# Products on 64 rows take turns between the two row halves of TensorE: attention scores by pairs of groups, selection scores, mixer scores

## The chip, the cores and the metric

One core of a Trainium2 chip runs the whole program in one launch. The time is the device time of one execution in microseconds (us), the median over runs. The engines have instruction streams of their own and run them in order: TensorE (PE, with a queue of weight loads beside its products), VectorE (DVE), ScalarE (ACT), GpSimd (POOL) and SyncE (SP). They meet at semaphores. Products are accumulated in PSUM, eight banks of 512 f32 columns by 128 partitions, and DVE or ACT carries them from there into SBUF.

## The reference, cut to what matters

The reference is a model of two blocks at 256 positions of width 1024. The first block has two layers: a mixer (a recurrence, attention with six heads and a position bias, and a state space part), then a layer that selects experts. The second has a recurrent mixer, an MLP, a sparse attention (NSA) with 16 heads in four groups, an MLP and a norm. Three kinds of product in it have 64 as the contracted dimension:

```python
# mixer attention: 6 heads of 64
s = jnp.einsum('bghnid,bghnjd->bghnij', qb, kw) + bias
# selection: 8 heads, each query in two halves of 64, each half against 128 sub-keys
q = (xt @ w_query).reshape(T, H, 2, PEER_HALF)
s = jnp.einsum('thcd,cnd->thcn', q, sub_keys)
sv, si = lax.top_k(s, K)
# NSA: 4 groups of 4 heads of 64; s_s (selected blocks) and s_w (window) for the same query
s_c = jnp.einsum('qghd,ngd->ghqn', qf, kc) - slopes * d_c      # 15 compressed keys
p_c = _masked_softmax(s_c, d_c >= 0)
s_s = jnp.einsum('qghd,gqkd->ghqk', qf, k_sel) - slopes * d_s
p_s = _masked_softmax(s_s, m_s)
s_w = jnp.einsum('qghd,kgd->ghqk', qf, kw) - slopes * d_w
p_w = _masked_softmax(s_w, m_w)
o = g[..., 0:1] * o_c + g[..., 1:2] * o_s + g[..., 2:3] * o_w
```

With 256 positions all four blocks of 64 are selected and the window holds everything, so that s_s and s_w are causal scores against two sets of keys.

## The kernel before, in words

Weights come as f32 from HBM, 512 KB at a time. ACT casts such a chunk to a high part (`hi`, L271), DVE subtracts it for the low part (`lo`, L273), and PE makes three products of each (`feat_mm`, L289, for results with features on partitions; `tok_mm`, L303, L305, L307, for results with tokens on partitions). This fills most of PE's time.

The program is written in an order of calls, and a list scheduler puts the instructions of each engine into the order in which they run. That order is fixed when the kernel is built. PSUM banks come from three pools: tag `a` (two banks), `acc` (four) and `g` (two). A tile of a pool gets its buffer when an earlier one is released.

Queries and keys lie with their features on partitions. Two heads (or two groups, or two halves of a query) share the 128 partitions: one on rows 0 to 63, the other on 64 to 127. A product on one half uses 64 rows of PE's array.

- **Mixer** (L671): for each token tile t of 128, the three even heads' scores into banks of `acc`, then the three odd heads'. DVE adds the bias (L673).
- **Selection** (`scores(t)`, L1046): for four heads at a time the first halves of their queries into one bank, then the second halves into the next. DVE then finds the 16 largest (L909 to L913).
- **NSA** (`attend(g, t)`, L1427): for a group g and a token tile t four heads' scores against two sets of keys, 256 columns a product for t=0 and 512 for t=1. They go into banks of tag `a`: two products a bank for t=0, one for t=1. DVE adds the position term (L1429) into the tile `ns` (three buffers), takes the maximum over keys (L1431), ACT takes eight exponentials (L1434), DVE multiplies by gate over sum (L1435 to L1439), PE transposes the result into banks of tag `g` (L1445), and ACT copies them to `pT` (L1447). `outputs(g)` multiplies them by the values (L1462, L1463), together with the compressed part (L1466).

Around it stand the calls of `nsa`: `query(i)` (24 products L289 with one weight chunk and a copy to `nq` on ACT, L1295) and `key`, `compressed(pr)` (scores against 15 compressed keys for eight heads: products L1384, softmax in the tile `sc`, weights `pc`, four transposes L1406, copy to `pcT` L1407), and `out(k)` (a weight chunk of the output, 12 products of `tok_mm`). A list `done` has the last exponential of each softmax; the high cast of a chunk of `query`, `key` and `out` is issued behind an entry of it:

```python
def project(i, tag=("a",)):
    if done: self.behind = done[-2:][:1]
    wh, wl = self.chunk(a["nsa_w_f"][i])
```

Of the kernel before, what the change touches and what calls it, by code (L numbers as in the profile page):

```python
# [16 lines left out]
OP = mybir.AluOpType  # L17
# [4 lines left out]
P = 128  # L22
# [159 lines left out]
class K:  # L182
# [446 lines left out]
    def attention(self, l, pool, u):  # L629
# [26 lines left out]
        for t in range(NT):  # L656
# [7 lines left out]
            for odd in range(2):  # L664
                rr = slice(odd * 64, odd * 64 + 64)
                for g0 in range(0, 3, per):
                    ng = min(per, 3 - g0)
                    b = self.bank("acc", 4)
                    for i in range(ng):
                        g = g0 + i  # L670
                        nc.tensor.matmul(b[:, i * w:(i + 1) * w], qkT[rr, g, t * P:(t + 1) * P], qkT[rr, 3 + g, :w],  # L671
                                         start=True, stop=True)
                    nc.vector.tensor_tensor(pv[:, g0:g0 + ng, odd], b[:, :ng * w].rearrange("p (h s) -> p h s", h=ng),  # L673
                                            rv[:, g0:g0 + ng, odd, S - w:], op=OP.add)
# [360 lines left out]
    def select(self, sp, qT, keys, sel, gates):  # L1035
# [4 lines left out]
        def scores(t):  # L1040
            banks = []
            for h4 in range(2):
                for c in range(2):
                    b = self.bank("acc", 4)
                    for j in range(4):
                        nc.tensor.matmul(b[:, j * P:(j + 1) * P], qT[c * 64:c * 64 + 64, 4 * h4 + j, t * P:(t + 1) * P],  # L1046
                                         keys[c * 64:c * 64 + 64, :], start=True, stop=True)
                    banks.append(b)
            return banks
# [215 lines left out]
    def nsa(self):  # L1265
# [3 lines left out]
        with tc.tile_pool(name="nsa", bufs=1) as pool:  # L1269
# [143 lines left out]
            def attend(g, t):  # L1413
                r = slice((g % 2) * 64, (g % 2) * 64 + 64)
                c0 = 4 * (g // 2)
                w = P * (t + 1)
                per = 512 // (2 * w)
                if t == 0:
                    for sb in range(2):
                        pT[g, sb] = T(f"pT{sb}", [P, 2, 4, S if sb == 0 else P], bufs=2)  # L1420
                s = T("ns", [P, 4, 2, S], bufs=3).rearrange("p h b s -> p (h b s)")[:, :8 * w].rearrange("p (h b s) -> p h b s", h=4, b=2)
                mx, sm = T("nmx", [P, 4, 2], bufs=3), T("nsm", [P, 4, 2], bufs=3)
                for h0 in range(0, 4, per):
                    b = self.bank("a")
                    bv = b.rearrange("p (h b s) -> p h b s", h=per, b=2)
                    for hh in range(h0, h0 + per):
                        nc.tensor.matmul(bv[:, hh - h0], qT[r, c0 + hh, t * P:(t + 1) * P], kT[r, g // 2, :, :w], start=True, stop=True)  # L1427
                    for hh in range(h0, h0 + per):
                        nc.vector.scalar_tensor_tensor(s[:, hh], alibi[:, None, S - w:].to_broadcast([P, 2, w]), slopes[4 * g + hh],  # L1429
                                                       bv[:, hh - h0], op0=OP.mult, op1=OP.add)  # L1430
# [6 lines left out]
                for hh in range(4):  # L1437
                    for br in range(2):
                        dv = nc.vector.tensor_scalar(s[:, hh, br], s[:, hh, br], sm[:, hh, br:br + 1], None, op0=OP.mult)  # L1439
                done.append((ex, dv if 0 else None))  # L1440
# [44 lines left out]
            compressed(0)  # L1485
            attend(0, 1)
            query(5)
            attend(1, 0)
            query(6)
            attend(1, 1)  # L1490
            outputs(0, ("acc", 4))
# [3 lines left out]
            attend(2, 0)  # L1495
# [3 lines left out]
            attend(2, 1)  # L1499
            out(1)  # L1500
            attend(3, 0)
            out(2)
            outputs(2, ("g",))
            attend(3, 1)
            out(3)
# [56 lines left out]
```

## Time and profile before

| | us |
|---|---|
| median of 3 runs | 2577.31 (2576.77 to 2577.53) |
| profiled execution | 2573.22 |
| its span, first to last instruction | 2571.4 |
| PE busy in it | 2493.8 (97%) |
| DVE busy | 1810.5 (70%) |
| ACT busy | 1202.0 (47%) |
| score products L1427 (NSA), L1046 (selection), L671 (mixer) | 64, 128 and 48 records |
| NSA, from the first L1427 to the L336 that close it | 104.83 |

A product of f32 tiles shows as two records of MATMUL in the trace. Busy time counts overlapping records once. A row of the timeline puts equal records one after another together: its start, the time until the last of them ends, their count, and in brackets how long the engine had been idle before the first of them and who ended that.

### The profile page before, as it was taken

The numbers are of one execution on the slowest core, as the hardware profiler recorded it, in microseconds if no ns is written. First come the engines' busy times: TensorE is split into PE (matmuls) and PEld (weight loads), VectorE is DVE, ScalarE is ACT, GpSimd is POOL, SyncE is SP. The second block draws the span as 40 slices with busy tenths as digits, with TensorE's granted clock in tenths as the row PEclk, the third lists the DMA queues.
The fourth block names the chain that finished last, engine by engine and source line by source line (L and its number), as shares of the span: only waits on it lengthen the run. The fifth ranks groups of instructions, "written<-read, shape, count | busy, mean of one in ns | idle before, by whom it ended". The sixth has DMA issues, their size and how long they took to land.

```text
span 2571.4 us, 44923 instructions
## 1 busy us (share of the span) xinstructions
PE 2493.8 (97%) x18200; PEld 2227.4 (87%) x18200; DVE 1810.5 (70%) x3138; ACT 1202.0 (47%) x1761; POOL 72.3 (3%) x79
## 2 busy tenths in 40 slices
PE   6999999999999998999999999999999999999998
PEld 5779999989978886889999989978879799886997
DVE  6768969964596557859968954696568655656655
ACT  5544443344434445544443444434447444455444
POOL 4000000000000003000000000000000000000000
PEclk9999999999999998999999999999999999999999
DMA  7235555465545664344554465545555555621564
GB/s 232 83 117 166 171 189 165 149 196 188 174 156 185 193 195 163 99 133 155 180 189 157 157 196 188 165 164 189 191 179 172 172 187 187 188 77 61 189 188 148
DMA packets 122072, 426.30 MB, mean 166 GB/s; under 512 B 14748, under 2 KB 18696, under 8 KB 121736
## 3 DMA queue, kind: packets, MB, share of 16 engines
q1 hardware_dynamic: 120448, 421.64, 51.3%
q8 instruction: 142, 2.33, 0.4%
q10 hardware_dynamic: 1416, 1.79, 0.2%
q14 instruction: 66, 0.54, 0.1%
HBM read 421.83 MB, written 2.24 MB: 165 GB/s over the span
## 4 chain that ended last, share of the span: by engine, by line
PE 48%; DVE 7%; ACT 1%; issue 1%; POOL 0%; DMA 0%; POOLq 0%; DVEq 0%; ACTq 0%
PE psa L289 19%; PE psacc L303 7%; PE psacc L307 7%; PE psacc L305 7%; DVE lo L273 2%; PE psacc L289 2%; PE psg L1004 1%; PE psa L1427 1%; PE psacc L300 1%; DVE tk L911 0%; PE psg L1445 0%; PE psacc L404 0%; DVE si L913 0%; ACT hi L271 0%; DVE x_sb L339 0%
## 5 line engine op out<-in xcount | busy, mean ns | idle before, releaser
L273 DVE TENSOR_TENSOR lo<-raw,hi 128x1024 fp32r<-128x1024 f32 (+1 forms) x778 | 942.7, 1219 | 494.1 <-ACT hi L271 493.6
L271 ACT CAST hi<-raw 128x1024 fp32r<-128x1024 f32 (+1 forms) x778 | 810.7, 1044 | 949.2 <-PE psa L289 512.0
L289 PE MATMUL psa<-xh,hi 128*128 128x256 f32 x2960 | 839.3, 288 | 2.4 <-DVE rst L241 1.7
L289 PE MATMUL psa<-xh,lo 128*128 128x256 f32 x2960 | 833.3, 285 | 2.4 <-DVE lo L273 2.3
L289 PE MATMUL psa<-xl,hi 128*128 128x256 f32 x2960 | 828.3, 283 | 0.0
L289 PEld LDWEIGHTS psa<-xh,hi 128*128 128x128 f32 x2960 | 569.4, 195 | 8.1 <-ACT xy L710 2.1
L289 PEld LDWEIGHTS psa<-xh,lo 128*128 128x128 f32 x2960 | 567.1, 193 | 6.1 <-DVE lo L273 5.6
L289 PEld LDWEIGHTS psa<-xl,hi 128*128 128x128 f32 x2960 | 563.8, 192 | 2.5
L303 PE MATMUL psacc<-hi,ch 128*128 128x512 f32 x984 | 305.6, 392 | 0.1
L305 PE MATMUL psacc<-lo,ch 128*128 128x512 f32 x984 | 303.6, 390 | 0.0
L307 PE MATMUL psacc<-hi,cl 128*128 128x512 f32 x984 | 302.8, 389 | 0.4 <-DVE cl L975 0.4
L307 PEld LDWEIGHTS psacc<-hi,cl 128*128 128x128 f32 x984 | 184.6, 188 | 40.1 <-DVE cl L975 1.2
L305 PEld LDWEIGHTS psacc<-lo,ch 128*128 128x128 f32 x984 | 184.7, 188 | 38.8
L303 PEld LDWEIGHTS psacc<-hi,ch 128*128 128x128 f32 x984 | 182.5, 188 | 36.3
L974 ACT CAST ch<-ca 128x512 fp32r<-128x512 f32 x124 | 77.0, 623 | 140.4 <-PE psacc L305 138.1
L975 DVE TENSOR_TENSOR cl<-ca,ch 128x512 fp32r<-128x512 f32 x124 | 85.7, 693 | 59.4 <-ACT ch L974 59.1
L1008 DVE TENSOR_TENSOR ca<-psg,ca 128x512 f32<-128x512 f32 x128 | 82.5, 688 | 15.2 <-PE psg L1004 15.2
L994 DVE TENSOR_TENSOR pg<-o,selg 128x1024 f16<-128x1024 f16 x128 | 82.8, 690 | 0.0
L376 POOL TENSOR_TENSOR ns<-ns,mhalf 128x1 f32<-128x1 f32 x18 | 15.9, 881 | 2231.4 <-DVE ns L375 2229.1
L989 DVE TENSOR_TENSOR o<-iota,sel 128x2048 f16<-128x2048 f16 x64 | 78.0, 1219 | 0.0
L303 PE MATMUL psacc<-hi,muh 128*128 128x512 f32 x248 | 77.3, 393 | 0.0
L305 PE MATMUL psacc<-lo,muh 128*128 128x512 f32 x248 | 76.8, 390 | 0.0
(411 smaller groups left out, 2663.9 us busy)
## 6 DMA issues: line engine op xcount, KB each, us to landing
raw<-in_down SPq DMA_DIRECT2D x256, 512.0 KB, 3.5
raw<-in_up SPq DMA_DIRECT2D x256, 512.0 KB, 3.5
raw<-in_mlp_up SPq DMA_DIRECT2D x64, 512.0 KB, 3.5
raw<-in_mlp_down SPq DMA_DIRECT2D x64, 512.0 KB, 3.5
raw<-in_w_in_t SPq DMA_DIRECT2D x32, 512.0 KB, 4.4
raw<-in_w_in_f SPq DMA_DIRECT2D x22, 512.0 KB, 4.3
raw<-in_w_out SPq DMA_DIRECT2D x16, 512.0 KB, 3.8
raw<-in_w_query SPq DMA_DIRECT2D x16, 512.0 KB, 3.5
```

Of the source, the lines that this page charges most:

```text
L271: nc.scalar.copy(hi, src)
L273: nc.vector.tensor_sub(lo, src, hi)
L289: nc.tensor.matmul(ps, w[:, k], x[:, k], start=i == 0, stop=i == len(seq) - 1)
L300: nc.tensor.matmul(acc[t][n][:, :w], xh[:, xs], wh[:, off[n]:off[n] + w], start=first, stop=last)
L303: nc.tensor.matmul(acc[t][n][:, :w], xh[:, xs], wh[:, off[n]:off[n] + w], start=first, stop=False)
L305: nc.tensor.matmul(acc[t][n][:, :w], xh[:, xs], wl[:, off[n]:off[n] + w], start=False, stop=False)
L307: nc.tensor.matmul(acc[t][n][:, :w], xl[:, xs], wh[:, off[n]:off[n] + w], start=False, stop=last)
L974: nc.scalar.copy(ch.rearrange("p b t -> p (b t)"), src)
L975: nc.vector.tensor_sub(cl.rearrange("p b t -> p (b t)"), src, ch.rearrange("p b t -> p (b t)"))
L989: nc.vector.tensor_tensor(pairs(o2), pairs(of(0, 64)), twice(si[:, 1], 64), op=OP.is_equal)
L994: nc.vector.tensor_tensor(pairs(pg[:, i]), pairs(o1), twice(sg[:, i], 32), op=OP.mult)
L1008: nc.vector.tensor_tensor(v, bk.rearrange("p (t i) -> p i t", t=8), v, op=OP.mult)
```

## The change

Mixer: one loop over the column groups, in which even and odd heads' products take turns, each half in a bank of its own. Selection: the same for the two halves of the queries. NSA: `attend(c, t)` now takes a pair of groups, 2c on rows 0 to 63 and 2c+1 on rows 64 to 127. Their products take turns into two banks of tag `a`; the additions on DVE follow, and then the two softmaxes, one after the other, in a function of their own. There are four calls of `attend` in place of eight, and the calls around it have another order. The amount of work is the same.

```diff
--- before.py
+++ after.py
@@ -661,16 +661,18 @@
             sm = pool.tile([P, 6], F32, tag="asm", name=self.nm("asm"), bufs=2)
             pv = p.rearrange("p (g two) s -> p g two s", two=2)
             rv = self.relb.rearrange("p (g two) s -> p g two s", two=2)
-            for odd in range(2):
-                rr = slice(odd * 64, odd * 64 + 64)
-                for g0 in range(0, 3, per):
-                    ng = min(per, 3 - g0)
-                    b = self.bank("acc", 4)
-                    for i in range(ng):
-                        g = g0 + i
-                        nc.tensor.matmul(b[:, i * w:(i + 1) * w], qkT[rr, g, t * P:(t + 1) * P], qkT[rr, 3 + g, :w],
+            for g0 in range(0, 3, per):
+                ng = min(per, 3 - g0)
+                bs = [self.bank("acc", 4) for _ in range(2)]
+                for i in range(ng):
+                    g = g0 + i
+
+                    for odd in range(2):
+                        rr = slice(odd * 64, odd * 64 + 64)
+                        nc.tensor.matmul(bs[odd][:, i * w:(i + 1) * w], qkT[rr, g, t * P:(t + 1) * P], qkT[rr, 3 + g, :w],
                                          start=True, stop=True)
-                    nc.vector.tensor_tensor(pv[:, g0:g0 + ng, odd], b[:, :ng * w].rearrange("p (h s) -> p h s", h=ng),
+                for odd in range(2):
+                    nc.vector.tensor_tensor(pv[:, g0:g0 + ng, odd], bs[odd][:, :ng * w].rearrange("p (h s) -> p h s", h=ng),
                                             rv[:, g0:g0 + ng, odd, S - w:], op=OP.add)
             nc.vector.tensor_reduce(mx, p, axis=AX.X, op=OP.max, negate=True)
             for h in range(6):
@@ -1040,12 +1042,13 @@
         def scores(t):
             banks = []
             for h4 in range(2):
-                for c in range(2):
-                    b = self.bank("acc", 4)
-                    for j in range(4):
-                        nc.tensor.matmul(b[:, j * P:(j + 1) * P], qT[c * 64:c * 64 + 64, 4 * h4 + j, t * P:(t + 1) * P],
+                bs = [self.bank("acc", 4) for _ in range(2)]
+                for j in range(4):
+
+                    for c in range(2):
+                        nc.tensor.matmul(bs[c][:, j * P:(j + 1) * P], qT[c * 64:c * 64 + 64, 4 * h4 + j, t * P:(t + 1) * P],
                                          keys[c * 64:c * 64 + 64, :], start=True, stop=True)
-                    banks.append(b)
+                banks += bs
             return banks
 
         ix = sp.tile([P, 2, NT, 8, 16], F32, tag="ix", name=self.nm("ix"))
@@ -1410,24 +1413,31 @@
             slopes = [2.0 ** (-8.0 * (h + 1) / 16) for h in range(16)]
             pT = {}
 
-            def attend(g, t):
-                r = slice((g % 2) * 64, (g % 2) * 64 + 64)
-                c0 = 4 * (g // 2)
+            def attend(c, t):
+
                 w = P * (t + 1)
                 per = 512 // (2 * w)
-                if t == 0:
-                    for sb in range(2):
-                        pT[g, sb] = T(f"pT{sb}", [P, 2, 4, S if sb == 0 else P], bufs=2)
-                s = T("ns", [P, 4, 2, S], bufs=3).rearrange("p h b s -> p (h b s)")[:, :8 * w].rearrange("p (h b s) -> p h b s", h=4, b=2)
+                ss = []
+                for g in (2 * c, 2 * c + 1):
+                    if t == 0:
+                        for sb in range(2):
+                            pT[g, sb] = T(f"pT{sb}", [P, 2, 4, S if sb == 0 else P], bufs=2)
+                    ss.append(T("ns", [P, 4, 2, S], bufs=3).rearrange("p h b s -> p (h b s)")[:, :8 * w].rearrange("p (h b s) -> p h b s", h=4, b=2))
+                for h0 in range(0, 4, per):
+                    bvs = [self.bank("a").rearrange("p (h b s) -> p h b s", h=per, b=2) for _ in range(2)]
+                    for hh in range(h0, h0 + per):
+                        for i in range(2):
+                            r = slice(i * 64, i * 64 + 64)
+                            nc.tensor.matmul(bvs[i][:, hh - h0], qT[r, 4 * c + hh, t * P:(t + 1) * P], kT[r, c, :, :w], start=True, stop=True)
+                    for i in range(2):
+                        for hh in range(h0, h0 + per):
+                            nc.vector.scalar_tensor_tensor(ss[i][:, hh], alibi[:, None, S - w:].to_broadcast([P, 2, w]),
+                                                           slopes[4 * (2 * c + i) + hh], bvs[i][:, hh - h0], op0=OP.mult, op1=OP.add)
+                for i in range(2):
+                    softmax(2 * c + i, t, ss[i])
+
+            def softmax(g, t, s):
                 mx, sm = T("nmx", [P, 4, 2], bufs=3), T("nsm", [P, 4, 2], bufs=3)
-                for h0 in range(0, 4, per):
-                    b = self.bank("a")
-                    bv = b.rearrange("p (h b s) -> p h b s", h=per, b=2)
-                    for hh in range(h0, h0 + per):
-                        nc.tensor.matmul(bv[:, hh - h0], qT[r, c0 + hh, t * P:(t + 1) * P], kT[r, g // 2, :, :w], start=True, stop=True)
-                    for hh in range(h0, h0 + per):
-                        nc.vector.scalar_tensor_tensor(s[:, hh], alibi[:, None, S - w:].to_broadcast([P, 2, w]), slopes[4 * g + hh],
-                                                       bv[:, hh - h0], op0=OP.mult, op1=OP.add)
                 nc.vector.tensor_reduce(mx, s, axis=AX.X, op=OP.max, negate=True)
                 for hh in range(4):
                     for br in range(2):
@@ -1436,8 +1446,8 @@
                 nc.vector.tensor_tensor(sm, sm, gv[:, t, 4 * g:4 * g + 4, 1:3], op=OP.mult)
                 for hh in range(4):
                     for br in range(2):
-                        dv = nc.vector.tensor_scalar(s[:, hh, br], s[:, hh, br], sm[:, hh, br:br + 1], None, op0=OP.mult)
-                done.append((ex, dv if 0 else None))
+                        nc.vector.tensor_scalar(s[:, hh, br], s[:, hh, br], sm[:, hh, br:br + 1], None, op0=OP.mult)
+                done.append((ex, None))
                 for br in range(2):
                     for sb in range(t + 1):
                         b = self.bank("g")
@@ -1483,26 +1493,22 @@
             attend(0, 0)
             query(4)
             compressed(0)
+            query(5)
             attend(0, 1)
-            query(5)
-            attend(1, 0)
             query(6)
-            attend(1, 1)
-            outputs(0, ("acc", 4))
             query(7)
             key(0, 1)
             key(1, 1)
-            attend(2, 0)
+            outputs(0, ("acc", 4))
+            attend(1, 0)
             outputs(1, ("acc", 4))
             out(0)
             compressed(1)
-            attend(2, 1)
             out(1)
-            attend(3, 0)
+            attend(1, 1)
             out(2)
+            out(3)
             outputs(2, ("g",))
-            attend(3, 1)
-            out(3)
             out(4)
             outputs(3, ("g",))
             out(5)
```

In what follows, names carry the tile's number: `psa`, `psacc` and `psg` are PSUM banks of tags `a`, `acc` and `g`. The first place is PE's stream at the beginning of the NSA scores. `ns_24258` and `ns_24261` are the t=0 score tiles of groups 0 and 1 after the change, `psa_24262` and `psa_24263` their first banks, `psa_24444` to `psa_24463` those of t=1. Before:

```order
L1427 MATMUL psa_24261<-nk_23687,nq_23686 128x256 x2
L1427 MATMUL psa_24266<-nk_23687,nq_23686 128x256 x2
L1427 MATMUL psa_24367<-nk_23687,nq_23686 128x512
L1427 MATMUL psa_24370<-nk_23687,nq_23686 128x512
L1427 MATMUL psa_24373<-nk_23687,nq_23686 128x512
L1427 MATMUL psa_24376<-nk_23687,nq_23686 128x512
L1427 MATMUL psa_24459<-nk_23687,nq_23686 128x256 x2
L1427 MATMUL psa_24464<-nk_23687,nq_23686 128x256 x2
```

Now:

```order
L1431 MATMUL psa_24262<-nk_23687,nq_23686 128x256
L1431 MATMUL psa_24263<-nk_23687,nq_23686 128x256
L1431 MATMUL psa_24262<-nk_23687,nq_23686 128x256
L1431 MATMUL psa_24263<-nk_23687,nq_23686 128x256
L1431 MATMUL psa_24272<-nk_23687,nq_23686 128x256 x2
L1431 MATMUL psa_24273<-nk_23687,nq_23686 128x256 x2
L1431 MATMUL psa_24444<-nk_23687,nq_23686 128x512
L1431 MATMUL psa_24445<-nk_23687,nq_23686 128x512
L1431 MATMUL psa_24450<-nk_23687,nq_23686 128x512
L1431 MATMUL psa_24451<-nk_23687,nq_23686 128x512
L1455 MATMUL psg_24303<-ident_sb,ns_24258 128x128
L1455 MATMUL psg_24309<-ident_sb,ns_24258 128x128
```

Before, group 0 has both its token tiles, then group 1 its first, and query products (L289) follow. Now the two groups take turns, with 24450 and 24451 one after the other, and eight transposes of group 0 stand behind, ahead of the remaining t=1 products.

The second place is ACT's stream there. `hi_24304` and `hi_24424` are the high casts of queries 4 and 5 before, `hi_24350` and `hi_24412` those after; `psacc_24416` is the bank of query 5 after. Before:

```order
L1434 ACTIVATE ns_24258,nsm_24260<-ns_24258,nmx_24259 128x128 x8
L271 CAST hi_24304<-raw_24302 128x1024
L271 CAST hi_24424<-raw_24422 128x1024
L1434 ACTIVATE ns_24364,nsm_24366<-ns_24364,nmx_24365 128x256 x7
L1447 COPY pT_3659_24256<-psg_24290 128x4x128
```

Now:

```order
L1444 ACTIVATE ns_24258,nsm_24283<-ns_24258,nmx_24282 128x128 x8
L1444 ACTIVATE ns_24261,nsm_24316<-ns_24261,nmx_24315 128x128 x6
L1457 COPY pT_3659_24256<-psg_24303 128x4x128
L1457 COPY pT_3659_24256<-psg_24309 128x4x128
L1444 ACTIVATE ns_24261,nsm_24316<-ns_24261,nmx_24315 128x128 x2
L271 CAST hi_24350<-raw_24348 128x1024
L271 CAST hi_24412<-raw_24410 128x1024
...
L1444 ACTIVATE ns_24442,nsm_24469<-ns_24442,nmx_24468 128x256 x2
L1298 ACTIVATE nq_23686<-psacc_24416 128x256
L1444 ACTIVATE ns_24442,nsm_24469<-ns_24442,nmx_24468 128x256 x5
L1395 ACTIVATE sc_24380<-sc_24380 128x240
```

The two casts stood behind eight exponentials and now stand behind sixteen and two copies. The exponential of the compressed scores (`sc_24380`) now stands behind the copy of query 5 and five exponentials of group 0's second token tile.

The third place is PE's stream around the transposes of the first `pc` tile. `psacc_24506` is the bank of query 6 before, `psacc_24416` that of query 5 after, `psacc_24564` that of query 6 after. Before:

```order
L289 MATMUL psacc_24506<-xh_23630,hi_24502 128x256
L289 MATMUL psacc_24506<-xl_23631,hi_24502 128x256
L289 MATMUL psacc_24506<-xh_23630,lo_24503 128x256
L1427 MATMUL psa_24538<-nk_23687,nq_23686 128x512
L1406 MATMUL psg_24358<-ident_sb,pc_24355 128x128 x4
L1445 MATMUL psg_24398<-ident_sb,ns_24364 128x128 x4
L1427 MATMUL psa_24541<-nk_23687,nq_23686 128x512
```

Now:

```order
L289 MATMUL psacc_24416<-xh_23630,hi_24412 128x256
L289 MATMUL psacc_24416<-xl_23631,hi_24412 128x256
L289 MATMUL psacc_24416<-xh_23630,lo_24413 128x256
L1409 MATMUL psg_24404<-ident_sb,pc_24401 128x128 x4
L1455 MATMUL psg_24489<-ident_sb,ns_24442 128x128 x4
L1455 MATMUL psg_24495<-ident_sb,ns_24442 128x128 x4
L1455 MATMUL psg_24501<-ident_sb,ns_24442 128x128 x4
L1455 MATMUL psg_24507<-ident_sb,ns_24442 128x128 x4
L1455 MATMUL psg_24534<-ident_sb,ns_24443 128x128 x3
L289 MATMUL psacc_24564<-xh_23630,hi_24560 128x256
L289 MATMUL psacc_24564<-xl_23631,hi_24560 128x256
```

Before, query 6's products stand ahead of these transposes; now query 5's do, and query 6's come behind them and behind 19 transposes of two groups.

## Rows read from the trace of the kernel before

**Rows 1.** The page: PE's busy time, and the chain that ended last, by engine.

```profile
PE 2493.8 (97%) x18200; PEld 2227.4 (87%) x18200; DVE 1810.5 (70%) x3138; ACT 1202.0 (47%) x1761; POOL 72.3 (3%) x79
...
PE 48%; DVE 7%; ACT 1%; issue 1%; POOL 0%; DMA 0%; POOLq 0%; DVEq 0%; ACTq 0%
```

**Rows 2.** Windows: stretch and length, busy us (instructions) by engine, PE clock, DMA.

```profile
core 0: us, PE busy (x) PEld busy (x) DVE busy (x) ACT busy (x) POOL busy (x), PEclk, DMA share, GB/s
2266.64:2314.16 47.52, 46.80 (x281) 36.36 (x280) 34.33 (x78) 32.00 (x93) 0.00 (x0) 0.93 0.23 73
2314.16:2371.47 57.31, 56.58 (x287) 39.08 (x287) 35.80 (x80) 31.14 (x90) 0.00 (x0) 0.97 0.22 69
...
2270.50:2273.20 2.70, 1.98 (x5) 0.66 (x4) 2.06 (x4) 2.49 (x13) 0.00 (x0) 0.99 0.00 0
2273.20:2280.00 6.80, 6.80 (x23) 5.56 (x23) 6.58 (x13) 6.13 (x20) 0.00 (x0) 0.50 0.17 48
2331.00:2334.60 3.60, 3.60 (x9) 2.19 (x8) 3.44 (x5) 0.40 (x1) 0.00 (x0) 0.53 0.00 1
```

**Rows 3.** Timeline of PE: NSA score products on one half, full clock.

```profile
2314.96 1.99 PE L1427 MATMUL psa<-nk,nq 64*128 64x256 f32 x8
...
2323.83 1.98 PE L1427 MATMUL psa<-nk,nq 64*128 64x512 f32 x4
```

**Rows 4.** Timeline of PE: selection burst; mixer, t=1, both halves, long and short window.

```profile
206.37 2.82 PE L1046 MATMUL psacc<-keys,qT 64*128 64x128 f32 x32
...
91.68 1.57 PE L671 MATMUL psacc<-aqkT 64*128 64x256 f32 x10
...
91.68 0.49 PE L671 MATMUL psacc<-aqkT 64*128 64x256 f32 x2
```

**Rows 5.** Timeline of PE: milestones of the first half of NSA.

```profile
2271.32 5.68 PE L1427 MATMUL psa<-nk,nq 64*128 64x512 f32 x12 [0.72 <-DVE ns L1429]
2276.93 0.58 PE L289 MATMUL psacc<-xh,hi 128*128 128x256 f32 x1
...
2280.27 0.27 PE L1445 MATMUL psg<-ident_sb,ns 128*128 128x128 f32 x1
...
2282.46 1.93 PE L1384 MATMUL psg<-kc,nq 128*128 128x30 f32 x16
...
2287.16 1.12 PE L1427 MATMUL psa<-nk,nq 64*128 64x512 f32 x2
...
2292.10 0.66 PE L1406 MATMUL psg<-ident_sb,pc 128*128 128x128 f32 x4
```

**Rows 6.** Timeline of DVE, the same stretch.

```profile
2267.80 1.62 DVE L1429 SCALAR_TENSOR_TENSOR ns<-alibi,psa 128x256 f32<-128x256 f32 x4 [7.37 <-PE psa L1427]
2269.45 1.22 DVE L1431 TENSOR_REDUCE nmx<-ns 128x8 f32<-128x1024 f32 x1
2270.59 1.27 DVE L1429 SCALAR_TENSOR_TENSOR ns<-alibi,psa 128x512 f32<-128x512 f32 x2
...
2274.11 2.29 DVE L1431 TENSOR_REDUCE nmx<-ns 128x8 f32<-128x2048 f32 x1
...
2278.72 1.65 DVE L1439 TENSOR_SCALAR ns<-ns,nsm 128x128 f32<-128x128 f32 x8
...
2288.90 0.41 DVE L1393 TENSOR_TENSOR sc<-sc,cmask 128x240 f32<-128x240 f32 x1 [0.97 <-ACT sc L1392]
...
2291.01 0.41 DVE L1401 TENSOR_TENSOR pc<-sc,cmx 128x240 f32<-128x240 f32 x1
```

**Rows 7.** Timeline of ACT, the same stretch: exponentials of 128 and 256, casts, copy.

```profile
2270.71 0.40 ACT L1434 ACTIVATE ns<-ns,nmx 128x128 f32<-128x128 f32 x1 [2.28 <-DVE nmx L1431]
...
2273.80 1.98 ACT L271 CAST hi<-raw 128x1024 fp32r<-128x1024 f32 x2
...
2276.94 0.49 ACT L1434 ACTIVATE ns<-ns,nmx 128x256 f32<-128x256 f32 x1
...
2287.04 0.38 ACT L1295 ACTIVATE nq<-psacc 128x256 f32<-128x256 f32 x1 [1.38 <-PE psacc L289]
...
2288.47 0.39 ACT L1392 ACTIVATE sc<-sc 128x240 f32<-128x240 f32 x1
```


## Prediction

> **What bounds the kernel now.** I read the page first, then the NSA attention stage by windows, then the timeline of each engine there. TensorE (PE) is busy 97% of the span, and the chain that ended last runs through it for 48%, through VectorE (DVE) for 7% [rows 1]. So PE time that goes away is gained, wherever nothing else is late instead. The profiled execution took 2573.2 us (span 2571.4), the median of the runs is 2577.3, 4.1 more. I work out differences and add them to the median; 0.2% of it, 5.2 us, is about what a measurement of this kernel can tell from no change.
>
> The change touches three places, and most of the products concerned stand in the NSA stage. From the first score product (2266.64) to the first of the closing output products (L336, 2371.47) it takes 104.83 us [rows 2]. PE is busy for 103.4 of these, so it idles 1.5; but in two stretches, of 6.8 and 3.6 us, the granted clock is 0.50 and 0.53 (the 1.2 GHz level), which costs about half of their length: 3.4 us in the first half of the stage and 1.7 in the second [rows 2]. Waits and clock together come to 6.6, and the work at full clock is 46.8 - 3.4 = 43.4 and 56.6 - 1.7 = 54.9, in sum 98.3. The reader is to see a stage in which PE hardly waits, though DVE and ACT work in it for only 70 and 63 us: query products fill PE while a softmax is under way.
>
> **What a pair of halves is worth.** On one row half a record of 256 columns follows the last after 0.215 us ((1.99 - 0.48) / 7), one of 512, by four in 1.98, after about 0.43; each product here is two records [rows 3]. For one of 128 columns I take half of the first, 0.11. The kernel before already changes halves in a few places, and there the records run side by side: two of 0.48 us take 0.49 together, and ten of 256 columns end after 1.57, where one behind another they would take 9 x 0.215 + 0.38 = 2.3 [rows 4]. So I take it that two products on different halves, in different banks and next to each other in the stream, cost one.
>
> **Selection scores.** Four bursts (two layers, two token tiles) of 32 records, now half after half: 2.82 us each [rows 4]. Alternating: 15 steps of 0.11 + 0.27 + 0.1 for the start = 2.0. Gain 0.75 each, **-3.0** in all (0 if DVE's top-16, which follows, sets the end; the feature products behind them on PE say no).
>
> **Mixer scores.** 48 records over two layers. In the second token tile half of them ran side by side already [rows 4]. At most 0.7 per tile; the order moves the products of the next branch ahead on PE by more than DVE delivers their inputs, so I take half of it less: 4 x 0.25 = **-1.0** (0 to -2).
>
> **NSA, overlap.** 32 products, 16 of 0.43 and 16 of 0.86 us: 20.6 us serial, at best 10.3 less. The order does not give all of it. Bank tag "a" has two banks; before, a bank was used again after its own group's DVE additions, now two banks at once wait for two groups. Side by side in PE's order stand the first four products of 256 columns (saves 0.86), 24444 with 24445 (0.86), 24456 with 24457 (0.86), and the one pair at the border of 24272 and 24273 (0.43); 24450 and 24451 come into the same bank one after another, so the second waits for the addition on the first. That is 3.0 per half of the stage, 6.0 in all.
>
> The Trainium skill speaks against more than this: "TensorEngine Tiling (Array Packing)", section "PSUM Bottleneck", says that tiling makes TensorE faster but not the evacuation of PSUM. The trace agrees: the addition that empties a 512-column bank takes 0.63 us on DVE [rows 6], longer than the 0.43 that a paired product would cost, and 16 of them are 10.1 us; by this rule alone the t=1 products cost 10.1 where 6.9 were hoped for.
>
> **NSA, new waits, first half.** Times run from the first score product. Before, ACT's first exponential starts at 4.07 [rows 7], the query products begin at 10.3 and the first transposes at 13.6 [rows 5].
> - DVE now does eight additions of 0.405 before any maximum: 0.7 + 3.2 + 1.1 (one reduction) = 5.1 to the first exponential. The second reduction (1.1) and the addition on 24444 (0.63) end at 6.9, and only then does PE get a bank for 24450 [rows 6]. Group 0's exponentials end at 5.1 + 8 x 0.385 = 8.2, its eight multiplications take 1.6, its transposes end about 11.6. Until there PE has 5.2 us of paired products and 1.0 of transposes: idle about 5.3 (before: 0.7) [rows 5].
> - Query products can't fill this, since their high casts stand on ACT behind 16 exponentials (6.2) and two copies (1.0), instead of behind eight: 5.1 + 6.2 + 1.0 + 1.9 for the two casts = 14.2, where before they ended at 9.1 [rows 7]. With the additions that hold back 24456 to 24463 another 1.9 of waiting. Query 5's products end at 11.6 + 11.3 of work (four products, 48 products of 0.12 (24 of them fill 2284.2 to 2287.1), eight transposes, the compressed scores 1.85) [rows 5] + 1.9 = 24.8.
> - There stand the transposes of pc (L1409), in PE's order directly behind query 5. Before, query 6 stood there, and L1406 ran at 25.5 without waiting [rows 5]. pc is made by: copy of query 5 on ACT (0.38), five exponentials of 0.49, the exponential of sc (0.39), then the DVE steps from the mask to pc, 2.5 in before (2288.90 to 2291.42) [rows 6, 7]. Sum **5.7 us** in which PE has nothing: everything behind L1409 waits, the 32 transposes and queries 6 and 7 too. Query 6's cast is on ACT behind the 16 exponentials, so a different order by chance won't fill it.
> - Behind L1409 36 transposes pass two banks of tag "g" at the pace of ACT's copies and of DVE's multiplications: about 2.5 more.
> Sum of waits 15.4. 43.4 - 3.0 + 15.4 = 55.8 against 47.5: **+8.3**.
>
> **Second half.** The same pair again. Additions hold back four of the products (0.9 + 0.9 + 0.9 + 0.5 = 3.2). At the second L1409 the last score product is followed by its addition (0.63), the reduction over 2048 elements (2.2) and the sc steps on DVE (2.5): 5.3. After it 1.8. 54.9 - 3.0 + 10.3 = 62.2 against 57.3: **+4.9**.
>
> **Clock.** Both halves are worked out at the full clock. The trace shows it fall right behind a stretch in which PE was busy for only 1.98 of 2.70 us [rows 2]; the holes now are longer. But at the lower level much of the work falls into time in which PE would wait anyway. I take **+1** (from -2, when it keeps its level, to +6, when another 7 us in the dense query products run at half).
>
> **Sum.** 8.3 + 4.9 + 1 - 3.0 - 1.0 = +10.2: 2577.3 + 10.2 = about **2587** (the profiled execution about 2583).
>
> **The rivals.**
> A (likeliest, 0.55): as worked out, 2583 to 2593.
> B (0.17): the holes are partly covered. The walk puts together rows measured in another order; where each wait is a third shorter (25.7 x 0.67) and the clock costs nothing, NSA is +3.6, the whole -0.4: 2577. For it: DVE and ACT have slack in the stage. Against: the 5.7 is a chain with every link on a row.
> C (0.15, the other sign): overlap as the rows show it gives 6 to 10.3 in NSA and 4 elsewhere, and PE waits no more than now. 2577.3 - 10.3 - 4 = 2563, with 6.0 2567. The mechanism is that ACT's casts arrive early enough for query products to fill the holes; it decides where waits and clock loss of the stage stay below 6.6 + 6.0 + 4.0 - 5.2 = 11.4 (mine: 26.7). For it: before does just this with 70 us of DVE work. Against: casts and pc stand behind twice as many exponentials in ACT's order. The Trainium skill would give it the whole 10.3: "TensorE: Matmul & The Clock Gate", section "Part 3: Packing small matmuls — row/col tiling", has packed products start about 4 ns apart; the 0.49 us for two agrees [rows 4].
> D (0.10): the change doesn't do what it says, because alternate halves run side by side only at a border and not in a long sequence. Then scores, mixers and NSA lose the 4 and up to 3 of the 6 (where DVE doesn't set the pace): 2587 + 7 = 2594. Against: the ten records [rows 4].
> The rest (0.03) is the clock at half over the query products, beyond 2597.
>
> **How the numbers follow.** Faster by over 0.2%: C and a little of B, 0.18. Within: most of B, 0.15. Slower: 0.67. Leaving out the far end of C and of the clock, the range is 2569 to 2598; A's own is 2583 to 2593.
>
> **What would show it.** PE idle some 5 us directly before each L1409, released by DVE's pc; idle of 4 to 5 us in the first 12 us of the stage, released by the additions L1434; the stage from the first L1431 to the L336 that close it at about 119 us; score bursts of about 2.0 us. I am wrong if PE's busy share in the stage stays at 98%, or if the query casts come before the exponentials of the second group.

## The result, and the profile after

The changed kernel takes 2599.56 us (median of 4 runs, 2595.49 to 2601.22), the kernel before 2577.04 beside it: ratio 1.0088, interval 1.0076 to 1.0101, so 19.6 to 26 us slower. I had forecast slower, 2587, in a range of 2569 to 2598: the sign was right, the size half of what came, and the time lies outside the range.

The profiled execution took 2595.49 us. NSA, from the first score product to the L336 that close it, grew from 104.83 [rows 2] to 124.78 us. The windows of the kernel after, whole stage first and then cut where the clock changes (columns as in [rows 2]):

```profile
2268.78:2393.56 124.78, 107.17 (x561) 76.57 (x561) 70.36 (x158) 62.16 (x182) 0.00 (x0) 0.88 0.18 60
...
2268.78:2277.70 8.92, 5.74 (x23) 2.78 (x22) 5.92 (x12) 4.82 (x19) 0.00 (x0) 0.98 0.00 0
2277.70:2294.20 16.50, 15.05 (x37) 8.24 (x38) 12.32 (x30) 6.56 (x23) 0.00 (x0) 0.50 0.17 64
2294.20:2304.60 10.40, 6.55 (x55) 6.34 (x54) 4.00 (x7) 5.76 (x22) 0.00 (x0) 0.99 0.00 1
2304.60:2310.60 6.00, 4.30 (x19) 3.59 (x20) 4.15 (x20) 5.69 (x20) 0.00 (x0) 0.51 0.01 3
...
2362.60:2369.00 6.40, 5.57 (x24) 4.31 (x24) 4.55 (x20) 5.93 (x18) 0.00 (x0) 0.51 0.00 0
```

The ledger of the stage comes from these rows. PE is busy for 107.17 and idle for 17.6 us (1.5 before). In the three stretches at the 1.2 GHz level it is busy for 15.05, 4.30 and 5.57; about half of that is lost, 7.5 + 2.1 + 2.7 = 12.3 (5.1 before). So the work at full clock is 94.9 (98.3 before). Idle time is +16.1, the clock +7.2, and what is left of the growth of 19.9, -3.4, I put down to the overlap of halves: it is a remainder and not measured by itself. With the stage cut into windows of 0.5 us, and busy time times granted clock added up over them, 13.4 us are lost to the clock and the work is 93.8; so the split between clock and overlap is good to about 1 us.

The timeline of PE after: two bursts of selection scores, then the first NSA score products and the rows before which PE idled longest (the number in brackets is the idle time before the row):

```profile
206.83 2.29 PE L1049 MATMUL psacc<-keys,qT 64*128 64x128 f32 x32
...
1208.62 2.06 PE L1049 MATMUL psacc<-keys,qT 64*128 64x128 f32 x32
...
2268.78 1.13 PE L1431 MATMUL psa<-nk,nq 64*128 64x256 f32 x8
2270.84 1.70 PE L1431 MATMUL psa<-nk,nq 64*128 64x256 f32 x8 [0.93 <-DVE ns L1434]
2272.78 1.79 PE L1431 MATMUL psa<-nk,nq 64*128 64x512 f32 x4 [0.24 <-DVE ns L1434]
2276.29 1.12 PE L1431 MATMUL psa<-nk,nq 64*128 64x512 f32 x2 [1.73 <-DVE ns L1434]
2278.19 2.07 PE L1431 MATMUL psa<-nk,nq 64*128 64x512 f32 x2 [0.78 <-DVE ns L1434]
...
2306.30 1.08 PE L1409 MATMUL psg<-ident_sb,pc 128*128 128x128 f32 x4 [5.55 <-DVE pc L1404]
...
2363.43 1.08 PE L1409 MATMUL psg<-ident_sb,pc 128*128 128x128 f32 x4 [5.31 <-DVE pc L1404]
```

Of the four bursts two take 2.29 us and two 2.06, beside 2.82 [rows 4]. The first NSA row (2268.78) shows what the change can give there: eight records of 256 columns end after 1.13 us, on one half they took 1.99 [rows 3]. The third (2272.78) shows why it rarely does: four of 512 take 1.79 beside 1.98. DVE's additions L1434 that empty the two banks run one behind the other (four from 2271.97 to 2273.38), so that the second bank came free later than the first. The last two are the holes before the transposes of pc, where the prediction put them.

ACT in the same stretch, from its timeline:

```profile
2274.55 0.40 ACT L1444 ACTIVATE ns<-ns,nmx 128x128 f32<-128x128 f32 x1 [3.98 <-DVE nmx L1441]
2283.73 1.98 ACT L271 CAST hi<-raw 128x1024 fp32r<-128x1024 f32 x2
2300.78 0.38 ACT L1298 ACTIVATE nq<-psacc 128x256 f32<-128x256 f32 x1 [3.17 <-PE psacc L289]
2303.52 0.39 ACT L1395 ACTIVATE sc<-sc 128x240 f32<-128x240 f32 x1
```

The first exponential starts 5.8 us into the stage (4.07 before [rows 7]), the two high casts end at 16.9 (9.1 before), and between the copy of query 5 and the exponential of sc five exponentials of a score tile pass.

### The profile page after: what moved, and what is told of

Read it like the earlier page. It is cut to its first block, busy times and chain, and to the rows that moved or that the text cites. A ratio compares the mean times of both kernels' runs of the same rounds, so it can differ in the third digit from the quotient of the medians.

```text
span 2593.7 us, 44922 instructions
## 1 busy us (share of the span) xinstructions
PE 2496.8 (96%) x18200; PEld 2227.6 (86%) x18200; DVE 1810.1 (70%) x3138; ACT 1201.9 (46%) x1761; POOL 72.9 (3%) x79
## 3 DMA queue, kind: packets, MB, share of 16 engines
q10 hardware_dynamic: 1416, 1.79, 0.2%
## 4 chain that ended last, share of the span: by engine, by line
PE 47%; DVE 7%; ACT 1%; issue 1%; POOL 0%; POOLq 0%; DVEq 0%; ACTq 0%
PE psa L289 19%; PE psacc L303 7%; PE psacc L307 7%; PE psacc L305 7%; DVE lo L273 2%; PE psacc L289 2%; PE psg L1006 1%; PE psa L1431 1%; PE psg L1455 1%; PE psacc L300 1%; DVE tk L913 0%; ACT hi L271 0%; DVE si L915 0%; PE psacc L404 0%; DVE ns L1434 0%
## 5 line engine op out<-in xcount | busy, mean ns | idle before, releaser
L289 PE MATMUL psa<-xh,hi 128*128 128x256 f32 x2960 | 839.8, 288 | 2.5 <-DVE rst L241 1.6
L289 PE MATMUL psa<-xh,lo 128*128 128x256 f32 x2960 | 834.6, 286 | 4.6 <-DVE lo L273 4.6
L289 PE MATMUL psa<-xl,hi 128*128 128x256 f32 x2960 | 829.1, 284 | 0.0
L289 PEld LDWEIGHTS psa<-xh,hi 128*128 128x128 f32 x2960 | 569.7, 195 | 8.3 <-ACT xh L409 2.1
L289 PEld LDWEIGHTS psa<-xh,lo 128*128 128x128 f32 x2960 | 567.9, 194 | 7.7 <-DVE lo L273 7.5
L289 PEld LDWEIGHTS psa<-xl,hi 128*128 128x128 f32 x2960 | 565.2, 193 | 2.5
```

Source lines behind the costliest of these rows:

```text
L289: nc.tensor.matmul(ps, w[:, k], x[:, k], start=i == 0, stop=i == len(seq) - 1)
```

## The experiments

Each was timed in turns with the kernel before on the same chip; the ratio is to that.

| run | what | ratio | interval |
|---|---|---|---|
| e1_scores | selection scores alone | 0.9989 | 0.9980 to 0.9998 |
| e2_nsa | NSA alone | 1.0073 | 1.0057 to 1.0088 |
| e3_order | NSA's order of calls, no pairs | 1.0037 | 1.0024 to 1.0050 |
| e4_nsa_free | NSA, query and key casts free | 1.0018 | 1.0009 to 1.0027 |
| e5_nsa_fill | NSA, first hole filled with repeats | 1.0096 | 1.0079 to 1.0113 |
| e6_nsa_free2 | NSA, all casts free | 1.0047 | 1.0029 to 1.0065 |
| e7_mixer | mixer alone | 1.0021 | 1.0012 to 1.0030 |
| e8_scores_mixer | scores and mixer | 1.0015 | 1.0007 to 1.0024 |
| e9_mixer_t0 | mixer, first token tile alone | 1.0033 | 1.0020 to 1.0046 |
| e10_mixer_t1 | mixer, second token tile alone | 1.0003 | 0.9993 to 1.0012 |
| e11_mixer_twice | mixer, every product twice | 1.0033 | 1.0021 to 1.0046 |
| e12_order_free | e3 with query and key casts free | 1.0028 | 1.0018 to 1.0038 |

**The parts.** e1, e2 and e7 are the three parts of the diff, each alone on the kernel before; e8 is two of them.

> The kernel before with the alternating selection scores alone. Theory (alternate halves run side by side, and VectorE's selection does not need the products sooner): each burst of 32 records falls from 2.82 to about 2.2 us, and the whole gets 1.5 to 3 us faster, 2574 to 2576 beside 2577. Rival (VectorE's top-16 behind the burst sets the end, so that the gain is given back within 10 us): bursts of 2.2 us and no change of the whole, within 0.5 us.

> The kernel before with the NSA part of the change alone (pairs of groups and the new order of calls; mixer and selection scores as before). Theory (all of the loss comes from the NSA stage): +19 to +21 us, some 2597, and the stage takes about 125 us with TensorE idle 5.5 and 5.3 us directly before the two transposes of pc. Rival (a part of the loss, some 4 us, comes from the mixer, where the changed kernel showed a stretch at half the clock around 1050 us): 2593 to 2595, with the stage still near 125.

> The kernel before with the alternating mixer scores alone. Theory (the six products of 128 columns and those of 256 run side by side, but what follows waits for VectorE anyway): each layer gains 0 to 0.5 us, the whole 0 to -1 us. Rival (the moved products open a wait for the next branch's inputs, 0.56 us in the changed kernel, and tip the clock to half in the second layer's mixer around 1050 us, where the changed kernel showed it for 6.8 us): +1 to +4 us.

> The kernel before with the alternating selection and mixer scores, NSA as before. Theory (the two are independent and the mixer's part is worth nothing): within 1 us of the scores alone, 2 to 3 us faster than before. Rival (the mixer's part costs 3 us or more): no faster than before.

0.11% of 2576 is 2.8 us faster for the scores, NSA costs 19 and the mixer 5.4: in sum +21 beside +22.7 for the whole. The theory that all the loss was in NSA fell: the mixer, counted at nothing, costs 3 to 8 us, and scores and mixer together (e8) are 2 to 6 us slower than before, so that the scores' gain doesn't make up for the mixer.

**The order of calls against the pairs.** e3 keeps the old `attend` and calls both groups of a pair one behind the other; e12 is the same with the line of e4 taken out.

```diff
-            attend(0, 0)
+            for g in (0, 1):
+                attend(g, 0)
             query(4)
             compressed(0)
+            query(5)
+            for g in (0, 1):
+                attend(g, 1)
...
```

> The kernel before with the new order of calls in NSA alone: both groups of a pair are called one after the other, each group's products, additions and softmax for itself as before. Theory (the pair's softmaxes one behind the other in the streams of VectorE and ScalarE make the holes, and the order of calls alone lets the scheduler keep query products in them): +3 to +8 us, no idle time of 5 us before the transposes of pc. Rival (the order of calls makes the loss, since queries 4 and 5 stand behind two softmaxes): +14 to +20 us, with the two holes of 5 us as in the changed kernel.

> The new order of calls with each group by itself, as before, and with the high casts of query and key weights not held behind an earlier softmax: the same as the kernel with pairs and free casts (2580), but without the pairs. It tells what the alternating halves in NSA are worth once the holes are filled. Theory (pairs save about 3 us of TensorE time, and their two softmaxes one behind the other cost a wait of 5 us before the second transposes of pc and its half clock, so that nothing is left): no hole of 5 us before either transposes of pc, the whole within 3 us of 2580 or up to 5 us faster. Rival (pairs pay once the casts are free): 3 to 8 us slower than 2580.

The order alone costs 9.5 us (6 to 13), half of what NSA costs, where the theory had 3 to 8. It makes no 5 us hole. At the beginning PE takes 14.6 us for 28 score records, with one wait of 0.78 us, the clock falls there, and the query products come behind them. PE's rows of e3, and the window from its first score product:

```profile
2269.26 3.96 PE L1427 MATMUL psa<-nk,nq 64*128 64x256 f32 x16
2274.01 9.85 PE L1427 MATMUL psa<-nk,nq 64*128 64x512 f32 x12 [0.78 <-DVE ns L1429]
...
2269.26:2285.00 15.74, 14.42 (x33) 6.59 (x32) 11.39 (x23) 10.41 (x38) 0.00 (x0) 0.66 0.00 0
```

Pairs add the other half (e2 against e3: 1.0073 and 1.0037, intervals apart), with the two holes. With free casts e12 has no 5 us hole and is at 1.0028, the pairs (e4) at 1.0018: the intervals overlap, so the times don't show a use of pairs in NSA either way. The stage by itself, from the first score product to the L336 that close it, says more, one profile of each kernel. Windows of e3, e2, e12 and e4:

```profile
2269.26:2385.34 116.08, 107.88 (x562) 76.97 (x562) 70.45 (x158) 62.31 (x182) 0.00 (x0) 0.90 0.20 64
2265.91:2391.65 125.74, 107.59 (x561) 76.08 (x561) 70.34 (x158) 62.03 (x182) 0.00 (x0) 0.86 0.18 59
2269.11:2380.66 111.55, 102.73 (x561) 74.21 (x561) 67.42 (x156) 60.64 (x180) 0.00 (x0) 0.97 0.19 62
2270.96:2379.16 108.20, 98.33 (x562) 70.51 (x561) 68.39 (x156) 60.20 (x180) 0.00 (x0) 0.97 0.19 64
```

Split by windows of 0.5 us, as above (casts held: issued behind an earlier softmax, as in the kernel before; free: without that line, as in e4):

| NSA stage, us | length | PE idle | lost to the clock | work at full clock |
|---|---|---|---|---|
| before | 104.83 | 1.5 | 5.1 | 98.3 |
| e3, new order, casts held | 116.08 | 8.2 | 10.5 | 97.4 |
| e2, new order, casts held, pairs | 125.74 | 18.2 | 13.2 | 94.4 |
| e12, new order, casts free | 111.55 | 8.8 | 3.3 | 99.4 |
| e4, new order, casts free, pairs | 108.20 | 9.9 | 2.5 | 95.8 |

Side by side, the pairs save 3.1 to 3.6 us of work in both cases. With the casts held they cost 10.0 of idle time and 2.7 of clock besides, and the stage is 9.7 longer; with the casts free only 1.0 of idle time, and the stage is 3.4 shorter. Seven profiles of kernels whose NSA is as before have the stage at 104.83 to 106.43, so 3.4 is more than that spread, but it rests on one execution of each. Freeing the casts takes 17.5 us off the stage with pairs and 4.5 without; no run frees them in the old order of calls.

**The casts.** e4 takes one line out of `project`, e6 the same line out of `out` too.

```diff
 def project(i, tag=("a",)):
-    if done: self.behind = done[-2:][:1]
     wh, wl = self.chunk(a["nsa_w_f"][i])
```

> As the kernel with the NSA part alone, but the high casts of query and key weights are not held behind an earlier softmax's last exponential (the line that sets behind in project is taken out). Theory (the first half loses because query casts come behind 16 exponentials, so that TensorE has nothing to do in the first 12 us and before the first transposes of pc): query products move into these holes, the hole before the first transposes of pc falls from 5.5 to about 1 us, the first half gets 9 to 13 us faster, the whole +6 to +10 instead of +20. Rival (the pair's scores are held by the additions on VectorE and the two banks of tag a, whatever the casts do): the first half stays 3 us within that of the NSA part alone, the whole +17 or more.

> As the kernel with the NSA part alone, but neither the high casts of query and key weights nor those of the output weights are held behind an earlier softmax's last exponential. Theory (the second hole of 5.3 us stays open because the output weights' casts come behind the pair's exponentials): output products move into it, the hole before the second transposes of pc falls to 2 us or less, the whole 2 to 5 us below the kernel in which only query and key casts are free (2580), that is 2575 to 2578. Rival (free casts get ahead of exponentials and additions on ScalarE and VectorE and make the pair's softmax itself late): the hole moves to the transposes of the pair's scores and the whole is 2580 or more.

e4 falls from 1.0073 to 1.0018, 14 us; it is at +4.6 (2.3 to 7.0), where +6 to +10 was expected. The stage in windows of e4, from the first score product to the first output product, up to the second transposes of pc, and behind these; the last line is from PE's timeline:

```profile
2270.96:2307.40 36.44, 33.51 (x229) 26.92 (x228) 28.05 (x64) 24.86 (x81) 0.00 (x0) 1.00 0.22 73
2307.40:2349.00 41.60, 34.76 (x177) 21.42 (x176) 27.72 (x69) 21.67 (x76) 0.00 (x0) 0.98 0.08 26
2349.00:2355.20 6.20, 6.09 (x26) 4.70 (x27) 4.35 (x17) 5.73 (x15) 0.00 (x0) 0.59 0.00 0
...
2349.08 1.09 PE L1405 MATMUL psg<-ident_sb,pc 128*128 128x128 f32 x4 [5.31 <-DVE pc L1400]
```

The clock stays at 1.00 through the first half, and the first transposes of pc come without a wait of their own. (The first score product starts at 2270.96 beside 2265.91 in e2. That comes from outside NSA: in this profile the clock fell in the first layer's mixer, and e4 is 5.4 us behind e2 already at the first selection burst. From the first score product on both have 145 records of query and key products L289.) The second half is as in e2: a wait of 5.31 before the second transposes, the clock at half behind it. e6 was to close it and did not. The wait fell to 3.60, but a second one came behind it, for the very cast that had been freed, which now stood in ACT's order behind the pair's 16 exponentials. PE in e6:

```profile
2356.01 1.08 PE L1405 MATMUL psg<-ident_sb,pc 128*128 128x128 f32 x4 [3.60 <-DVE pc L1400]
2364.03 2.17 PE L1451 MATMUL psg<-ident_sb,ns 128*128 128x128 f32 x8 [2.58 <-ACT hi L271]
```

Here the rival was right: by the ratios e6 takes 7 us more than e4, with intervals apart.

**The clock behind a hole.** e5 makes query 5's products twice more, into banks that nobody reads.

```diff
-            query(5)
+            query(5, 2)
...
+                for _ in range(again):
+                    self.feat_mm(self.bank(*tag)[:, :S], v3(wh), v3(wl), xh, xl)
```

> As the kernel with the NSA part alone, with query 5's 24 products made twice more into banks that nobody reads: 48 products of 0.12 us, 5.8 us of added work, which stand in TensorE's order in the hole of 5.55 us before the first transposes of pc. Theory (the hole costs twice: the wait itself, and the clock at half behind it, 6.8 us long): the products fill the hole, the transposes of pc come at the same time to within 0.5 us, the granted clock behind them stays at 1.0, and the first half gets 2 to 3.4 us faster although work was added. Rival (the fall of the clock does not hang on the idle time): first half the same or up to 1 us slower, the half clock at the same place.

Windows of e5, of the filled hole and the stretches behind it, then one of e2, from its first transposes of pc:

```profile
2300.00:2306.00 6.00, 6.00 (x51) 5.90 (x50) 3.35 (x14) 5.53 (x23) 0.00 (x0) 1.00 0.01 1
2306.00:2310.20 4.20, 2.99 (x22) 2.20 (x21) 1.43 (x6) 4.10 (x13) 0.00 (x0) 1.00 0.00 0
2310.20:2314.20 4.00, 2.55 (x13) 2.58 (x13) 3.42 (x11) 3.30 (x5) 0.00 (x0) 0.67 0.00 0
...
2304.59:2310.59 6.00, 6.00 (x27) 4.62 (x27) 4.15 (x17) 5.69 (x16) 0.00 (x0) 0.54 0.01 3
```

PE is busy through the hole, and the clock behind it stays at 1.00 where e2, the same kernel without the repeats, shows 0.54 for 6 us. In e2 the clock falls inside the hole, 1 us before the transposes of pc (2303.3), for 7 us; in e5 it falls 5 us behind them (2311.3), for 3 us, behind new waits: the scheduler had moved the next casts, and PE waited 2.22 us for one. So in these two profiles the fall moves with the idle time. The expected gain of 2 to 3.4 us did not come: from the first score product to the first output product e5 takes 59.5 us, e2 57.9, and the whole is no better (1.0096). The run doesn't size the clock's part by itself.

**The mixer.** e9 and e10 alternate in one token tile only, e11 issues each product twice. The edit of e11, against e7:

```diff
-                    for odd in range(2):
+                    for odd in (0, 1, 0, 1):
```

> The kernel before with alternating mixer scores for the first token tile only. Theory (the loss of the mixer's part, about 5 us, comes from here: the shorter burst lets the scheduler put the next branch's products, which wait 0.56 us for VectorE, directly behind it, and 9 us later the clock falls to half for 6.8 us in nearly every execution instead of in a part of them): +3 to +6 us, the wait of 0.5 us and the half clock from about 91 and 1050 us in the trace. Rival (the order of the second token tile's products makes the clock fall): within 1.5 us of before.

> The kernel before with alternating mixer scores for the second token tile only. Theory (the loss comes from the first token tile): within 1.5 us of before, no wait of 0.5 us behind the first burst. Rival (the second token tile's order makes the clock fall): +3 to +6 us with the half clock from about 91 and 1050 us.

> The kernel before with alternating mixer scores in which every one of the products is made twice, so that a burst keeps TensorE as long as one half behind the other would (the second time writes the same values). Theory (TensorE's time is not what costs; with bursts of the old length the wait for the next branch's inputs is covered, and the clock falls no more often than before): within 1.5 us of before, no wait of 0.5 us behind the burst. Rival (added work costs its own time, or the interleaving of halves itself lowers the clock): +4 us or more.

The first token tile costs 8.5 us (1.0033); for the second no cost can be told from nothing (1.0003, -1.8 to +3.1 us). The row of PE's timeline in e9 behind the first burst:

```profile
82.52 0.60 PE L745 MATMUL psg<-upto,sda 128*6 128x256 f32 x2 [0.56 <-DVE sda L742]
```

And windows of e9 in the two layers' mixers:

```profile
88.00:106.00 18.00, 18.00 (x173) 15.31 (x174) 7.71 (x17) 8.81 (x35) 0.00 (x0) 0.72 0.10 30
1044.00:1064.00 20.00, 19.44 (x222) 15.52 (x219) 13.50 (x28) 9.52 (x37) 0.00 (x0) 0.83 0.26 80
```

18 us at 0.72 and 20 at 0.83 are 5.0 + 3.4 = 8.4 us of clock. That the profiled span is just 8.4 above that of before is partly chance, but most of it does come up in these stretches: e9 is behind the kernel before by 5.3 us at the first selection burst (211.64 beside 206.37 [rows 4]) and by 7.7 at the first NSA score product (2274.29 beside 2266.64). The fall is not new. In nine profiles whose mixer's first tile is as before (the kernel before, e1 to e6, e10, e12), 5 of the 18 mixers show it; in the four with the alternating first tile (after, e7, e8, e9) 7 of 8. So the change makes frequent what happened now and then. What tips it isn't settled, but the 0.56 us wait alone doesn't: the kernel after has it in its first layer and stays at 1.00 there from 88 to 106, and e1 falls without it. e11, which was to show that the wait does it, failed. That wait fell to 0.16, but in the first layer the moved order made another of 2.13 us at 100 and the clock fell right behind it; in the second, with no wait above 0.28 in the 9 us in front, the clock fell all the same, for 3 us. The whole is as slow as e9.

## Why the prediction was right in sign and short in size

- **Selection, -3.0:** right. Bursts went from 2.82 to 2.29 and 2.06, where I had 2.0, which is 2.6 us in all; alone the part gives -2.8 (interval -5.2 to -0.5).
- **Mixer, -1.0 (0 to -2):** wrong in sign. Alone it costs 3.1 to 7.7 us. The step that failed is "the order moves the products of the next branch ahead on PE by more than DVE delivers their inputs, so I take half of it less". The move and its wait were seen (0.56 us), but I priced them as the wait alone. The runs show in its place that the clock falls 9 us later in 7 of 8 mixers, 5.0 and 3.4 us lost in e9; why it does stays open.
- **NSA, overlap, -6.0:** -3.4 as a remainder, -3.1 from e3 to e2. I counted pairs as side by side where the order has them next to each other. But the second bank comes free one addition later, so that of 24444 and 24445 only 0.2 us overlapped, not 0.86. "TensorEngine Tiling (Array Packing)" of the Trainium skill, section "PSUM Bottleneck", says that evacuation does not get faster with tiling; here that held more strictly than I took it. Idle time before the score products that DVE's additions ended went from 6.6 to 18.4 us, PE and its weight loads counted together (1.0 and 6.1 for PE alone). The views of one line's waits, L1427 before and L1431 after:

```profile
  DVE ns L1429: 6.6, 10
...
  DVE ns L1434: 18.4, 22
```

- **NSA, waits, 25.7:** 17.6. The two holes before pc were right to 0.2 us (5.7 and 5.3 forecast, 5.55 and 5.31 seen), with the releaser named and, in the timelines of ACT and DVE, the links as I had them. The waits on additions in the first 12 us were about 3.7 where I had 5.3: products that overlapped less, and ran at half the clock from 2277.7 on, stood where I had idle time.
- **NSA, clock, "I take +1":** the step that failed most. My sum took out the 5.1 us that before loses to the clock and set the loss after the change at 1 us; it was 12.3 (13.4 by the finer windows). The reason, that "at the lower level much of the work falls into time in which PE would wait anyway", did not hold: the first fall lasted 16.5 us with PE busy for 15.05 of them. The range for it (to +6) was too short too. I had the place right ("the holes now are longer") and not the length, for which the row of before, 6.8 us behind a hole of 0.7, was no bound.
- Of the three NSA terms the error is +11.3 for the clock, -8.1 for the waits, +2.6 for the overlap: +5.8 net, from +14 to +20. That the clock and the waits erred in opposite directions is luck. The mixer adds 6.4. Together that is the 12 us between 2587 and 2599.6.
- **Rivals.** D (no side-by-side) is out: the bursts and the first row of NSA show it. C's condition, casts that come early enough, was not met here; e4 makes it so for the first half, and then 14 of the 19 us are gone, though it still doesn't win. B had waits a third shorter, 17.2, and they came to 17.6, but not by covering of the two holes, and its clock "costs nothing" was 12.3. (B's sum has a slip: 98.3 - 6.0 + 17.2 is 4.7 above 104.83, not 3.6, and the whole about 2578.) The time fell into what I called the rest, at 0.03: the clock at half, beyond 2597, only over score products more than over query products, and with the mixer's part.
- **Best version.** The selection scores alone, 0.9989: faster than both kernels, by 2.8 us, with an interval that ends just below 1.

## What to carry to other kernels

In this kernel two products side by side saved their time only where two destinations were free at once (1.13 us beside 1.99); where one engine emptied them in turn, little was left of it (1.79 beside 1.98), and the softmax behind each pair came in a lump that left PE without fill. Before you regroup, look at what stands in the other engines' in-order streams ahead of the fill. Here it was weight casts: with them held the pairs made the stage 9.7 us longer, with them free 3.4 shorter. And where rows of before show the clock fall behind short waits, price any longer wait with the clock behind it (here 2.1 to 7.5 us lost behind one wait or a row of them), and don't take a small edit as free because its own term is small.

## What the runs showed of the hardware that I had not expected

The clock can fall in the mixers' stretch without a wait in front and without a change there. e1 has the mixer of before; its clock falls at 91.2 for 6.8 us, PE's timeline lists no wait from 78 on, and PE is busy in all of the 5 us in front, much of it with products of 32 and 64 columns (L563). Its window of the first layer reads

```profile
88.00:106.00 18.00, 18.00 (x172) 15.44 (x171) 8.39 (x19) 10.42 (x37) 0.00 (x0) 0.81 0.09 31
```

while the same window of the kernel before has PE busy for 17.08 us at 1.00. The Trainium skill's page "TensorE: Matmul & The Clock Gate", section "Part 1: The HAM clock gate (the "warmup" mystery)", has the slow clock as the state at rest, which activity releases. The filled hole of e5 agrees, with the clock at 1.00 behind it; for the mixers no run here shows what released or withheld it.
